# A hybrid decoder block: order of the up projection's first products, slots for value weights, three stages for down's weight sums, and down's first operands during up

## The chip, the cores and the metric

The kernel runs on one core of one Trainium2 chip. The metric is device time in microseconds, the median of several executions. Five engines work beside each other: TensorE (PE) multiplies and transposes, ScalarE (ACT) and VectorE (DVE) work elementwise, GpSimd (POOL) takes a few subtractions, and SyncE (SP) issues all transfers in its own order. Each engine takes its instructions in program order.

## What is computed

One decoder block on 1024 rows of width 1024, in float32:

```python
h = rms_norm(x, norm_mix_w)
q_nsa, kv_nsa, g_nsa, q_ret, k_ret, v_ret, g_ret, g_merge = jnp.split(h @ w_in, split_at, axis=-1)
y_a = nsa_attention(...) @ w_nsa_branch                  # 512 -> 1024
y_b = gated_norm(retention(...)) @ w_ret_branch          # 1024 -> 1024
gate_a, gate_b = jnp.split(jax.nn.sigmoid(g_merge), 2, axis=-1)
x = x + (gate_a * y_a + gate_b * y_b) @ w_mix_out        # 1024 -> 1024
h = rms_norm(x, norm_ffn_w)
u = causal_dwconv(h @ w_ffn_up)                          # 1024 -> 2 x 2816, width 3
u_gate, u_val = jnp.split(u, 2, axis=-1)
x = x + (jax.nn.silu(u_gate) * u_val) @ w_ffn_down       # 2816 -> 1024
return rms_norm(x, norm_final_w)
```

## The kernel before, in words

**Splits.** Every matrix product is made of three products of two parts: `split` (L175, L176) makes a high part on ScalarE (a copy into the product's type) and a low part on VectorE or GpSimd (source minus high part). High by high, high by low and low by high are added up in PSUM (`mm3`, L283 in the profile). A weight block is 128 x 1024 floats, 512 KB; it is loaded into `wr`, a buffer with two slots (`wraw`), and split into `wh` and `wl` (`wpool`, five slots of each).

**Order.** A scheduler sets the order of each engine from the program, as far as data and buffer slots allow; only TensorE's order from the second half of mix to the first products of up is the order of the code (`pe_order`).

**Branch stage.** The loop over `ch` and `i` (L1000 to L1018) makes eight attention rows: the gate row `gated(j)` (L978, a load; L979, a sigmoid) is multiplied on VectorE with the row's product (L1012), and the retention output is transposed and split into `orT`. A second loop does the same for eight retention rows with `w_b`, adds the attention rows `ma` and splits the sum into `mh`, `ml`.

**Sums of down's weights.** Up and down are each done with seven products of halves instead of eight (a Winograd form), which needs sums of operands. `t_sums(j, x, y)` makes those of down's weights for step j of 11: four loads of 256 KB (L989, L990) into `tq`, four subtractions on VectorE (L992 to L995), four stores (L997) to `t0` to `t3` in device memory. Before, six of the 11 stand in the attention rows, five in the first half of mix.

**Mix.** Two halves of `w_mix` in four weight blocks each (`Weights`: L202 load, L209 high part, L215 low part). In the second half each finished row is normalised (`end_row`), and `piece` transposes it and copies it (L1087, L1090), makes its low part (L1091) and, for rows 4 to 7, the sums of halves (L1098 to L1101, two of the four on GpSimd but in the last row).

**Up.** 22 filters f, each with seven products of 512 columns in a row of banks. `sums` splits the row sums into `bht`, `blt` (L175, L176). The first five filters (`LEAD`) begin early: `first_weights` loads and splits the gate half of a filter's weights, `start_up` multiplies it and copies the product (L1186, `c` from `f`), and only then the next product may be added to that bank. `other_weights` loads the value half and makes sums of both halves on VectorE (L1214 to L1220). `up` does the other products; `conv` (L1230 on ScalarE, L1231 and L1232 on VectorE) convolves the two results, and their product (L1259) is stored (L1261) as `act`.

**Down.** Units (product i, step j) take activations `a` (two loads L1290, split `sh`, `sl`) and weights. `prepared` fetches both, two units ahead. The tail is not touched by the change, but that `a11` is loaded once more.

Of the kernel before, what the change touches and what calls it, by code (L numbers as in the profile page):

```python
# [18 lines left out]
P = 128  # L19
D = 1024  # L20
S = 1024
# [142 lines left out]
def hybrid_block(ctx: ExitStack, tc: tile.TileContext, a, c, out):  # L164
# [839 lines left out]
    for ch in range(2):  # L1004
        nx = Weights(w_a, 0, 4, [(512, 512)]) if ch == 0 else Weights(w_b, 0, KT, [(0, 512)])
        for i in range(4):
# [7 lines left out]
            if len(t_left) > 5:  # L1014
                x, y = ([q[:, 0:512], q[:, 512:S]] for q in
                        (mp.tile([P, S], F32, name="tq", tag="gb", bufs=3) for _ in range(2)))
                t_sums(t_left.pop(0), x, y)
            transposed_split(ps1, o_r[ch * 4 + i], *orT, ch * 4 + i)  # L1018
        gw = nx
    with ort:  # L1020
# [8 lines left out]
        for ch in range(2):  # L1029
            nx = Weights(w_b, 0, KT, [(512, 512)]) if ch == 0 else Weights(w_mix, 0, KT, [(0, 512)])  # L1030
            for i in range(4):
# [10 lines left out]
                ml.append(mlj)  # L1042
            gw = nx
# [34 lines left out]
    def piece(t, h):  # L1078
# [43 lines left out]
    for t in range(NT):  # L1122
        residual(t, 0)
        if t in (1, 3, 5, 6, 7) and len(t_left):
# [42 lines left out]
    def raw_up(f, i):  # L1167
        r = wraw.tile([P, 2, 512], F32, name="wr")
        nc.sync.dma_start(r.rearrange("p a b -> p (a b)"), a["w_ffn_up"][f][:, i * 1024:(i + 1) * 1024])
        return r  # L1170

    def first_weights(f):

        g = raw_up(f, 0)
        p = parts2(g, nc.gpsimd)
        return {k: [x[:, i] for x in p] for i, k in enumerate(("a11", "a12"))}, g
# [26 lines left out]
    cpool = ups.enter_context(tc.tile_pool(name="cp", bufs=8, reuse_waits="tile"))  # L1203
# [6 lines left out]
    def other_weights(f, w, g=None):  # L1210
        v = raw_up(f, 1)
        g = g or raw_up(f, 0)
# [22 lines left out]
    def up(f, w, begun=None):  # L1235
        x, p1 = begun or start_up(w)
# [12 lines left out]
        if not begun:  # L1249
            prod(x, w["a12"], "21", False, True)  # L1250
# [12 lines left out]
    def weights(f):  # L1263
        if f in uw:
            return other_weights(f, uw.pop(f))
        return other_weights(f, *first_weights(f))

    nx = weights(0)
# [7 lines left out]
    STEPS = [(j, min(2, HT - j)) for j in range(0, HT, 2)]  # L1276
    NS = len(STEPS)
# [5 lines left out]
    W = {"b11": (0, 0), "b21": (1, 0), "b22": (1, 1)}  # L1283
    A = {"a11": (0, 0), "a12": (1, 0), "a21": (0, 1), "a22": (1, 1)}
    kept = {}

    def fetch_a(k, i, dst):
# [3 lines left out]
        return dst  # L1291

# [33 lines left out]
    def prepared(sk, tk, i):  # L1326
        j, n = STEPS[i]
        t = wraw.tile([P, 2, 512], F32, name="wr")
        if tk in W:
            kh, nh = W[tk]  # L1330
            r0 = (kh * HT + j) * P
            src = w_dn[r0:r0 + n * P, nh * 512:nh * 512 + 512].rearrange("(k p) n -> p k n", p=P)
        else:
            src = t_d[int(tk[1]) - 1][j:j + n].rearrange("k p n -> p k n")
# [153 lines left out]
```

## Time and profile before

| | us |
|---|---|
| median of 3 executions | 1814.02 (1811.32 to 1814.24) |
| profiled execution | 1812.5 |
| its span in the trace | 1810.7 |
| TensorE busy | 1750.6 |
| VectorE busy | 1186.5 |
| ScalarE busy | 804.2 |
| GpSimd busy | 126.6 |

The span is what the trace covers of the profiled execution. TensorE has work in nearly all of it, so the views to read are those that tell where it has none: its instructions with the idle time ahead of each and the instruction that ended it. All times below are microseconds from the span's start.

### The profile page before, as it was taken

The numbers are of one execution on the slowest core, as the hardware profiler recorded it, in microseconds if no ns is written. First come the engines' busy times: TensorE is split into PE (matmuls) and PEld (weight loads), VectorE is DVE, ScalarE is ACT, GpSimd is POOL, SyncE is SP. The second block draws the span as 40 slices with busy tenths as digits, with TensorE's granted clock in tenths as the row PEclk, the third lists the DMA queues.
The fourth block names the chain that finished last, engine by engine and source line by source line (L and its number), as shares of the span: only waits on it lengthen the run. The fifth ranks groups of instructions, "written<-read, shape, count | busy, mean of one in ns | idle before, by whom it ended". The sixth has DMA issues, their size and how long they took to land.

```text
span 1810.7 us, 22500 instructions
## 1 busy us (share of the span) xinstructions
PE 1750.6 (97%) x8331; PEld 1434.6 (79%) x8331; DVE 1186.5 (66%) x2337; ACT 804.2 (44%) x1464; POOL 126.6 (7%) x78
## 2 busy tenths in 40 slices
PE   7999999999999999999989999789999999999998
PEld 6987888888788888888868877667888888878886
DVE  7445877777875554455644446767767777678666
ACT  6334666666662344136332215434444444343344
POOL 0000020110100000000000002301121211000000
PEclk9999999999999999999989999899999999999999
DMA  6121010110202111101682383322322322395353
GB/s 227 55 82 53 19 56 32 36 59 18 71 24 94 47 37 57 47 1 47 231 270 93 93 300 137 99 70 70 104 71 82 93 70 87 108 354 189 94 163 111
DMA packets 87418, 178.88 MB, mean 99 GB/s; under 512 B 8508, under 2 KB 18316, under 8 KB 87308
## 3 DMA queue, kind: packets, MB, share of 16 engines
q1 hardware_dynamic: 87308, 177.44, 30.2%
q8 instruction: 65, 1.06, 0.2%
q14 instruction: 45, 0.37, 0.1%
HBM read 137.57 MB, written 39.85 MB: 98 GB/s over the span
## 4 chain that ended last, share of the span: by engine, by line
PE 60%; DVE 5%; DMA 4%; ACT 2%; issue 2%; SPq 1%; POOL 1%; DVEq 0%; POOLq 0%; ACTq 0%
PE f L283 33%; PE mm L283 19%; PE fill L772 2%; DMA tq<-in_w_ffn_down 2%; PE po L826 1%; PE pv L718 1%; PE pt L706 1%; PE sc L610 1%; DMA wr<-in_w_ffn_up 1%; PE pst L826 1%; DMA wr<-in_w_mix_out 0%; ACT wh L209 0%; PE pss L871 0%; DVE c L1231 0%; DVE c L1232 0%
## 5 line engine op out<-in xcount | busy, mean ns | idle before, releaser
L283 PE MATMUL mm<-wh,hh 128*128 128x512 f32 (+1 forms) x576 | 224.0, 389 | 0.5 <-ACT hh L175 0.5
L283 PE MATMUL mm<-wh,hl 128*128 128x512 f32 (+1 forms) x576 | 219.8, 382 | 0.0
L283 PE MATMUL mm<-wl,hh 128*128 128x512 f32 (+1 forms) x576 | 219.8, 382 | 0.0
L209 ACT ACTIVATE wh<-wr 128x1024 fp32r<-128x1024 f32 (+1 forms) x72 | 74.6, 1037 | 167.0 <-PE mm L283 83.2
L713 DVE TENSOR_TENSOR pl<-pt,ph 128x512 fp32r<-128x512 f32 (+1 forms) x148 | 100.6, 686 | 41.8 <-ACT ph L710 41.2
L283 PEld LDWEIGHTS mm<-wh,hl 128*128 128x128 f32 x576 | 108.8, 189 | 20.6 <-DVE hl L176 0.3
L283 PEld LDWEIGHTS mm<-wh,hh 128*128 128x128 f32 x576 | 108.8, 189 | 20.2 <-ACT hh L175 0.9
L283 PE MATMUL f<-wh,sh 128*128 128x512 f32 x308 | 121.6, 395 | 3.3 <-ACT sh L175 3.3
L710 ACT ACTIVATE ph<-pt 128x512 fp32r<-128x512 f32 (+1 forms) x148 | 87.7, 594 | 82.8 <-PE pt L706 74.5
L283 PEld LDWEIGHTS mm<-wl,hh 128*128 128x128 f32 x576 | 108.9, 189 | 19.5 <-DVE wl L215 0.5
L283 PE MATMUL f<-wl,sh 128*128 128x512 f32 x308 | 121.5, 395 | 0.0
L283 PE MATMUL f<-wh,sl 128*128 128x512 f32 x308 | 120.7, 395 | 0.0
L283 PE MATMUL f<-bh,wh 128*128 128x512 f32 x264 | 105.0, 398 | 11.9 <-ACT c L1186 11.9
L176 POOL TENSOR_TENSOR wl<-wr,wh 128x1024 fp32r<-128x1024 f32 x22 | 53.6, 2438 | 898.3 <-ACT wh L175 883.4
L283 PE MATMUL f<-bht,wh 128*128 128x512 f32 x264 | 104.8, 397 | 8.3 <-ACT wh L175 8.3
L772 PE MATMUL fill<-hh,wh 128*128 128x512 f32 x256 | 104.5, 408 | 3.0 <-ACT sg L784 2.0
L283 PE MATMUL f<-bht,wl 128*128 128x512 f32 x264 | 105.0, 398 | 2.2 <-DVE wl L176 2.2
L628 ACT ACTIVATE big<-big,st 128x640 f32<-128x640 f32 (+7 forms) x128 | 93.4, 730 | 28.1 <-DVE st L624 27.3
L215 DVE TENSOR_TENSOR wl<-wr,wh 128x1024 fp32r<-128x1024 f32 (+1 forms) x60 | 71.5, 1193 | 51.2 <-ACT wh L209 50.2
L283 PE MATMUL f<-blt,wh 128*128 128x512 f32 x264 | 104.4, 395 | 0.0
L283 PE MATMUL f<-bl,wh 128*128 128x512 f32 x264 | 104.1, 394 | 0.0
L283 PE MATMUL f<-bh,wl 128*128 128x512 f32 x264 | 103.4, 393 | 0.0
(282 smaller groups left out, 4127.6 us busy)
## 6 DMA issues: line engine op xcount, KB each, us to landing
wr<-in_w_ffn_up SPq DMA_DIRECT2D x49, 512.0 KB, 4.7
wr<-in_w_in SPq DMA_DIRECT2D x40, 512.0 KB, 3.7
tq<-in_w_ffn_down SPq DMA_DIRECT2D x44, 256.0 KB, 4.7
t<-tq SPq DMA_DIRECT2D x44, 256.0 KB, 3.0
act<-c SPq DMA_DIRECT2D x22, 512.0 KB, 2.8
wr<-t SPq DMA_DIRECT2D x20, 512.0 KB, 3.5
a<-act SPq DMA_DIRECT2D x33, 256.0 KB, 6.0
gate<-sg SPq DMA_DIRECT2D x32, 256.0 KB, 2.0
```

The lines of the kernel that those rows point to most:

```text
L176: (engine or nc.vector).tensor_tensor(lo, src, f32(hi), OP.subtract)
L209: nc.scalar.activation(hi[:, :, :self.n], self.raw[len(self.hi)], AF.Copy)
L215: self.engine.tensor_tensor(lo[:, :, :self.n], self.raw[j], f32(self.hi[j][:, :, :self.n]), OP.subtract)
L283: nc.tensor.matmul(ps, stat(sp, kt), mov(mp, kt), start=(first and n == 0), stop=(last and n == 3 * nk - 1), skip_group_check=more)
L610: nc.tensor.matmul(out[:, c0:c0 + n], q[:, h, :], mov, start=(q is box["h"]), stop=(q is box["l"]))
L628: nc.scalar.activation(probs[b][h], probs[b][h], AF.Exp, scale=-1.0, bias=stat["nm", b][:, h:h + 1], accum_out=stat["w", b][:, h:h + 1])
L706: nc.tensor.transpose(bx["pt"][:rows, h, :], probs[h][:, k * P:k * P + rows], ident)
L710: nc.scalar.activation(bx["h"][:rows], bx["pt"][:rows], AF.Copy)
L713: nc.vector.tensor_tensor(bx["l"][:rows], bx["pt"][:rows], f32(bx["h"][:rows]), OP.subtract)
L718: nc.tensor.matmul(acc["pv"], v, bx[part][:rows].rearrange("p h q -> p (h q)"), start=start, stop=stop)
L772: nc.tensor.matmul(fx["ps"], w.at(sp, kt, i * P, P), hT[mp][:, kt, half * 512:half * 512 + 512], start=(n == 0), stop=(n == 3 * KT - 1))
L826: nc.tensor.matmul(ps[:, h, :], stat[sp][:, h, :], mov[mp][:, h, :], start=(first and n == 0), stop=(last and n == 2))
```

## The change

It has four parts. The sums of down's weights are made in three stages: four in the attention rows (even rows), three in the retention rows (j = 2, 4, 6, in buffers of attention rows already added), four in the first half of mix. The splits of the row sums of up stand behind the loop of the first five filters in the program, and `piece` makes all four subtractions on VectorE. The value half of up's weights gets a buffer of its own (`v`, two slots), the general buffer `c4` has 6 slots for 8; the second sum is made in place in `wr`, and filters 5 to 21 load their gate half a second time for it. The operands of down's unit (0, 0) are loaded and split before the last filter of up, through `wr` and `wh`, `wl`; the first step of `a11` is loaded again for the third product.

```diff
-            if len(t_left) > 5:
+            if (ch * 4 + i) % 2 == 0:
...
+                if j in (2, 4, 6):
+                    x, y = ([q[:, 0:512], q[:, 512:S]] for q in
+                            (mp.tile([P, S], F32, name="tq", tag=f"ma{j - k}") for k in (2, 1)))
+                    t_sums(t_left.pop(0), x, y)
...
-        side = nc.vector if t == NT - 1 else nc.gpsimd
         nc.vector.tensor_tensor(b11, b12, b11, OP.subtract)
-        side.tensor_tensor(b12, b22, b12, OP.subtract)
+        nc.vector.tensor_tensor(b12, b22, b12, OP.subtract)
         nc.vector.tensor_tensor(b22, b22, b11, OP.subtract)
-        side.tensor_tensor(b21, b21, b22, OP.subtract)
+        nc.vector.tensor_tensor(b21, b21, b22, OP.subtract)
...
-        if t in (1, 3, 5, 6, 7) and len(t_left):
+        if t in (0, 1, 2, 4):
...
-    sums([4, 5])
-    uw, begun = {}, {}
+    fw, begun = {}, {}
     for f in range(LEAD):
-        uw[f], _ = first_weights(f)
-        begun[f] = start_up(uw[f])
+        fw[f] = first_weights(f)
+        begun[f] = start_up(fw[f])
         if f in (0, 2):
-            t = waiting[0][0]
             piece(*waiting.pop(0))
-            sums([t])
-        prod(begun[f][0], uw[f]["a12"], "21", False, True)
+        prod(begun[f][0], fw[f]["a12"], "21", False, True)
+    sums([4, 5, 6])
+    sums([7])
...
-    cpool = ups.enter_context(tc.tile_pool(name="cp", bufs=8, reuse_waits="tile"))
+    cpool = ups.enter_context(tc.tile_pool(name="cp", bufs=6, reuse_waits="tile"))
...
-        v = raw_up(f, 1)
-        g = g or raw_up(f, 0)
+        v = cpool.tile([P, 2, 512], F32, name="v", bufs=2)
+        nc.sync.dma_start(v.rearrange("p a b -> p (a b)"), a["w_ffn_up"][f][:, 1024:])
+        g = raw_up(f)
...
-        s2 = c4()
-        nc.vector.tensor_sub(s2[:, 0], g[:, 0], v[:, 0])
-        nc.vector.tensor_sub(s2[:, 1], g[:, 1], s[:, 1])
-        p = parts2(s2, nc.vector)
+        nc.vector.tensor_sub(g[:, 0], g[:, 0], v[:, 0])
+        nc.vector.tensor_sub(g[:, 1], g[:, 1], s[:, 1])
+        p = parts2(g, nc.vector)
...
+    ready = {}
+    nx = other_weights(0)
     for f in range(FT):
-        w, nx = nx, weights(f + 1) if f + 1 < FT else None
-        up(f, w, begun.pop(f, None))
+        w, nx = nx, None
+        if f + 1 < FT:
+            if f + 1 >= LEAD:
+                fw[f + 1] = first_weights(f + 1)
+            nx = other_weights(f + 1)
+        if f == FT - 1:
+            s = fetch_a("a11", 0, wraw.tile([P, 2, 512], F32, name="wr"))
+            ready[0, 0] = [parts2(s, nc.vector), parts2(fetch_t("b11", 0), nc.vector)]
+        up(f, w)
...
-    ready = {}
...
         if i == 1:
+            held("a11", j)
             held("a21", j)
             held("a22", j)
```

`fetch_t` holds the weight load that stood in `prepared`; `STEPS`, `W`, `A` and `fetch_a` stand earlier in the program and are otherwise the same.

**What moves in the order, 1.** SyncE's queue in the attention rows. `ma4`, `ma5` and `ma6` are the gate loads of the fifth, sixth and seventh row (from `gate4` to `gate6`), `tq` the loads of sums, `t0` to `t3` their stores, `wr` weight blocks of the retention rows. Before:

```order
L202 DMA wr_8790<-in_w_ret_branch 128x2x512
L978 DMA ma4_8796<-gate4_1647 128x1024
L997 DMA t2_8525<-tq_8744 128x512
L989 DMA tq_8825<-in_w_ffn_down 128x512
L997 DMA t1_8524<-tq_8745 128x512
L997 DMA t3_8526<-tq_8745 128x512
L990 DMA tq_8825<-in_w_ffn_down 128x512
L989 DMA tq_8826<-in_w_ffn_down 128x512
L990 DMA tq_8826<-in_w_ffn_down 128x512
L978 DMA ma5_8853<-gate5_1648 128x1024
```

With the change:

```order
L202 DMA wr_8756<-in_w_ret_branch 128x2x512
L978 DMA ma4_8768<-gate4_1647 128x1024
L202 DMA wr_8762<-in_w_ret_branch 128x2x512
L989 DMA tq_8797<-in_w_ffn_down 128x512
L990 DMA tq_8797<-in_w_ffn_down 128x512
L989 DMA tq_8798<-in_w_ffn_down 128x512
L990 DMA tq_8798<-in_w_ffn_down 128x512
L978 DMA ma5_8825<-gate5_1648 128x1024
L997 DMA t0_8523<-tq_8797 128x512
L978 DMA ma6_8868<-gate6_1649 128x1024
```

Between the fifth and the sixth row's gate stood three stores and four loads of two different sums; now there are four loads of one, and the seventh gate follows behind one store.

**What moves in the order, 2.** ScalarE at the start of up. `c2` from `f` is the copy of the first product (L1186 before, L1188 now), `bht` from `pc` are the splits of sums, `wh` from `wr` that of a weight block, `rs_s` and `h` belong to the last row's norm. Before:

```order
L175 ACTIVATE bht2_10398<-pc_10282 128x4x128
L175 ACTIVATE bht2_10398<-pc_10351 128x4x128
L256 ACTIVATE h_10373,ss_10374<-c2_10324 128x512
L175 ACTIVATE bht3_10400<-pc_10275 128x4x128
L233 ACTIVATE rs_s_10379<-rs_v_10377 128x1
L175 ACTIVATE bht3_10400<-pc_10344 128x4x128
L175 ACTIVATE bht1_10402<-pc_10007 128x4x128
L175 ACTIVATE bht1_10402<-pc_10074 128x4x128
L175 ACTIVATE bht4_10404<-pc_10016 128x4x128
L175 ACTIVATE bht4_10404<-pc_10083 128x4x128
L1186 ACTIVATE c2_10441<-f_10428 128x512
```

With the change:

```order
L175 ACTIVATE bht2_10396<-pc_10280 128x4x128
L175 ACTIVATE wh_10492<-wr_10490 128x1024
L256 ACTIVATE h_10371,ss_10372<-c2_10322 128x512
L175 ACTIVATE bht2_10396<-pc_10349 128x4x128
L175 ACTIVATE bht3_10398<-pc_10273 128x4x128
L233 ACTIVATE rs_s_10377<-rs_v_10375 128x1
L1188 ACTIVATE c2_10423<-f_10410 128x512
```

The copy stands ahead of five splits that it followed, and behind one split of weights (`wh_10492`) that was not there.

**What moves in the order, 3.** VectorE at the step from up to down. L1255 (now L1257) ends the last filter's last product, L1231 and L1232 (now L1233 and L1234) are its convolutions, L1259 (now L1261) their product; `sl` are low parts of down's activations, `wl` of its weights. Before:

```order
L1255 TENSOR_TENSOR c4_13476<-f_13463,c2_13446 128x512
L176 TENSOR_TENSOR wl_13671<-wr_13661,wh_13670 128x1024
L176 TENSOR_TENSOR sl_13563<-a11_0_13559,sh_13562 128x1024
L1231 SCALAR_TENSOR_TENSOR c4_13518<-c4_13476,cw_65,c4_13518 128x1023
L1231 SCALAR_TENSOR_TENSOR c4_13523<-c4_13477,cw_65,c4_13523 128x1023
L1232 SCALAR_TENSOR_TENSOR c4_13518<-c4_13476,cw_65,c4_13518 128x1022
L1232 SCALAR_TENSOR_TENSOR c4_13523<-c4_13477,cw_65,c4_13523 128x1022
L176 TENSOR_TENSOR sl_13576<-a11_1_13572,sh_13575 128x1024
L1259 TENSOR_TENSOR c4_13518<-c4_13518,c4_13523 128x1024
```

With the change:

```order
L1257 TENSOR_TENSOR c4_13499<-f_13486,c2_13469 128x512
L176 TENSOR_TENSOR wl_13644<-wr_13634,wh_13643 128x1024
L1233 SCALAR_TENSOR_TENSOR c4_13541<-c4_13499,cw_65,c4_13541 128x1023
L1233 SCALAR_TENSOR_TENSOR c4_13546<-c4_13500,cw_65,c4_13546 128x1023
L1234 SCALAR_TENSOR_TENSOR c4_13541<-c4_13499,cw_65,c4_13541 128x1022
L1234 SCALAR_TENSOR_TENSOR c4_13546<-c4_13500,cw_65,c4_13546 128x1022
L176 TENSOR_TENSOR sl_13586<-a11_1_13582,sh_13585 128x1024
L1261 TENSOR_TENSOR c4_13541<-c4_13541,c4_13546 128x1024
```

The low part of step 0 is gone from this place; that of step 1 stands behind the convolutions, as before.

## Rows read from the trace of the kernel before

**Rows 1.** The page, part 1: engine, busy us, share of the span, instructions.

```profile
PE 1750.6 (97%) x8331; PEld 1434.6 (79%) x8331; DVE 1186.5 (66%) x2337; ACT 804.2 (44%) x1464; POOL 126.6 (7%) x78
```

**Rows 2.** TensorE by line, 880 to 960: count | busy, mean | idle before, releaser.

```profile
L283 PE MATMUL mm<-oaT,wh 128*128 128x512 f32 x107 | 35.5, 413 | 2.2 <-DVE ma L1012 2.2
...
L283 PE MATMUL mm<-orT,wh 128*128 128x512 f32 x58 | 21.6, 451 | 2.6 <-DVE ma L1012 2.6
...
L275 PE MATMUL tp<-ident,big 128*128 128x128 f32 x56 | 7.9, 286 | 3.0 <-DVE orT L176 3.0
```

**Rows 3.** Table by stretches: length, busy time (instructions) by engine, PEclk, DMA share, GB/s.

```profile
880.00:920.00 40.00, 35.70 (x175) 29.08 (x174) 27.22 (x37) 14.74 (x22) 0.00 (x0) 0.93 0.91 307
920.00:960.00 40.00, 36.47 (x134) 27.23 (x133) 15.31 (x17) 9.37 (x10) 0.00 (x0) 0.86 0.64 219
960.00:1030.00 70.00, 70.00 (x310) 57.91 (x309) 31.98 (x27) 19.89 (x19) 0.00 (x0) 1.00 0.24 78
1060.00:1090.00 30.00, 27.08 (x118) 21.46 (x117) 16.61 (x29) 6.93 (x12) 0.00 (x0) 1.00 0.90 304
1125.00:1150.00 25.00, 14.89 (x55) 11.60 (x54) 22.56 (x31) 13.40 (x25) 13.22 (x8) 0.80 0.25 81
1185.00:1240.00 55.00, 44.51 (x173) 33.73 (x172) 41.05 (x48) 21.71 (x23) 4.12 (x3) 0.94 0.26 87
1240.00:1585.00 345.00, 345.00 (x1496) 280.35 (x1494) 252.33 (x287) 147.50 (x160) 60.53 (x34) 1.00 0.27 86
```

**Rows 4.** Timeline of SyncE's queue, branch stage: start, us of issuing.

```profile
917.53 0.45 SPq L978 DMA_DIRECT2D ma<-gate  x1
```

**Rows 5.** Timeline of TensorE, mix stage: start, us, [idle before, releaser].

```profile
1078.68 0.49 PE L283 MATMUL f<-wh,mh 128*128 128x512 f32 x1 [2.15 <-ACT wh L209]
```

**Rows 6.** Timeline of VectorE, mix stage.

```profile
1069.30 0.69 DVE L993 TENSOR_TENSOR tq<-tq 128x512 f32<-128x512 f32 x1 [4.67 <-DMA tq<-in_w_ffn_down]
```

**Rows 7.** TensorE, start of up: by line from 1125 to 1185, then timeline.

```profile
L283 PE MATMUL f<-bh,wh 128*128 128x512 f32 x44 | 19.3, 438 | 11.9 <-ACT c L1186 11.9
...
1136.29 0.80 PE L283 MATMUL f<-bh,wh 128*128 128x512 f32 x1 [7.04 <-ACT c L1186]
...
1146.69 0.80 PE L283 MATMUL f<-bh,wh 128*128 128x512 f32 x1 [3.07 <-ACT c L1186]
```

**Rows 8.** Timeline of ScalarE, start of up.

```profile
1130.34 0.63 ACT L175 ACTIVATE bht<-pc 128x512 fp32r<-128x512 f32 x1 [4.25 <-DVE pc L1100]
...
1133.07 2.69 ACT L175 ACTIVATE bht<-pc 128x512 fp32r<-128x512 f32 x5
1135.67 0.57 ACT L1186 ACTIVATE c<-f 128x512 f32<-128x512 f32 x1
```

**Rows 9.** Timeline of GpSimd and of VectorE, start of up.

```profile
1123.42 2.42 POOL L176 TENSOR_TENSOR wl<-wr,wh 128x1024 fp32r<-128x1024 f32 x1 [1.02 <-ACT wh L175]
...
1129.61 0.69 DVE L1100 TENSOR_TENSOR pc<-pc 128x512 f32<-128x512 f32 x1 [0.85 <-POOL pc L1099]
```

**Rows 10.** TensorE by line, first filters of up, 1185 to 1240.

```profile
L283 PE MATMUL f<-bht,wh 128*128 128x512 f32 x38 | 15.6, 411 | 8.3 <-ACT wh L175 8.3
L283 PE MATMUL f<-bht,wl 128*128 128x512 f32 x37 | 15.2, 412 | 2.2 <-DVE wl L176 2.2
```

**Rows 11.** Timeline of VectorE, one filter of up.

```profile
1418.82 1.22 DVE L1259 TENSOR_TENSOR c<-c,c 128x1024 f32<-128x1024 f32 x1
...
1437.74 1.22 DVE L1259 TENSOR_TENSOR c<-c,c 128x1024 f32<-128x1024 f32 x1
...
1442.61 1.22 DVE L176 TENSOR_TENSOR wl<-c,wh 128x1024 fp32r<-128x1024 f32 x1
```

**Rows 12.** Timeline of TensorE and of VectorE, first unit of down.

```profile
1588.50 0.50 PE L283 MATMUL f<-wh,sh 128*128 128x512 f32 x1 [3.26 <-ACT sh L175]
...
1589.62 2.48 DVE L1231 SCALAR_TENSOR_TENSOR c<-c,cw,c 128x1023 f32<-128x1023 f32 x2
```

**Rows 13.** The page, part 6: loads of up's weights, count, KB, median us to landing.

```profile
wr<-in_w_ffn_up SPq DMA_DIRECT2D x49, 512.0 KB, 4.7
```

More of the change, by code (lines that the diff above doesn't have):

```diff
@@ L1165, in parts2, with raw_up @@
         return hi, lo
-    def raw_up(f, i):
+    def raw_up(f):
         r = wraw.tile([P, 2, 512], F32, name="wr")
-        nc.sync.dma_start(r.rearrange("p a b -> p (a b)"), a["w_ffn_up"][f][:, i * 1024:(i + 1) * 1024])
+        nc.sync.dma_start(r.rearrange("p a b -> p (a b)"), a["w_ffn_up"][f][:, 0:1024])
         return r
     def first_weights(f):
-        g = raw_up(f, 0)
-        p = parts2(g, nc.gpsimd)
-        return {k: [x[:, i] for x in p] for i, k in enumerate(("a11", "a12"))}, g
+        p = parts2(raw_up(f), nc.gpsimd)
+        return {k: [x[:, i] for x in p] for i, k in enumerate(("a11", "a12"))}
     def prod(ps, w, k, first=True, last=True):
@@ L1208, in hybrid_block, with other_weights @@
     act_d = [dram.tile([P, 2, 512], F32, name=f"act{f}") for f in range(FT)]
-    def other_weights(f, w, g=None):
-        v = raw_up(f, 1)
-        g = g or raw_up(f, 0)
+    def other_weights(f):
+        w = {}
+        v = cpool.tile([P, 2, 512], F32, name="v", bufs=2)
+        nc.sync.dma_start(v.rearrange("p a b -> p (a b)"), a["w_ffn_up"][f][:, 1024:])
+        g = raw_up(f)
         s = c4()
@@ L1233, in conv, with up @@
         return y
-    def up(f, w, begun=None):
-        x, p1 = begun or start_up(w)
+    def up(f, w):
+        x, p1 = begun.pop(f, None) or start_up(fw[f])
         y = bank()
@@ L1248, in up @@
         nc.vector.tensor_add(cv[:, 1], z, u3)
-        if not begun:
-            prod(x, w["a12"], "21", False, True)
+        if f >= LEAD:
+            prod(x, fw[f]["a12"], "21", False, True)
         nc.scalar.activation(cg[:, 0], x, AF.Copy)
@@ L1261, in up, with fetch_a, fetch_t @@
         nc.sync.dma_start(act_d[f], yg)
[L1263 to L1268, printed above, removed]
-    for f in range(FT):
-        w, nx = nx, weights(f + 1) if f + 1 < FT else None
-        up(f, w, begun.pop(f, None))
+    STEPS = [(j, min(2, HT - j)) for j in range(0, HT, 2)]
+    NS = len(STEPS)
+    A = {"a11": (0, 0), "a12": (1, 0), "a21": (0, 1), "a22": (1, 1)}
+    W = {"b11": (0, 0), "b21": (1, 0), "b22": (1, 1)}
+    def fetch_a(k, i, dst):
+        (kh, sh), (j, n) = A[k], STEPS[i]
+        for x in range(n):
+            nc.sync.dma_start(dst[:, x], act_d[kh * HT + j + x][:, sh])
+        return dst
+    def fetch_t(k, i):
+        j, n = STEPS[i]
+        t = wraw.tile([P, 2, 512], F32, name="wr")
+        if k in W:
+            kh, nh = W[k]
+            r0 = (kh * HT + j) * P
+            src = w_dn[r0:r0 + n * P, nh * 512:nh * 512 + 512].rearrange("(k p) n -> p k n", p=P)
+        else:
+            src = t_d[int(k[1]) - 1][j:j + n].rearrange("k p n -> p k n")
+        nc.sync.dma_start(t[:, :n], src)
+        return t
+    ready = {}
+    nx = other_weights(0)
+    for f in range(FT):
+        w, nx = nx, None
[7 more added lines that the diff above has]
+        up(f, w)
     tp.close()
     ups.close()
-    STEPS = [(j, min(2, HT - j)) for j in range(0, HT, 2)]
-    NS = len(STEPS)
     keep = ctx.enter_context(tc.tile_pool(name="keep", bufs=1, side="right", reuse_waits="tile"))
@@ L1282, in hybrid_block @@
     kp2 = ctx.enter_context(tc.tile_pool(name="keep2", bufs=1, reuse_waits="tile"))
-    W = {"b11": (0, 0), "b21": (1, 0), "b22": (1, 1)}
-    A = {"a11": (0, 0), "a12": (1, 0), "a21": (0, 1), "a22": (1, 1)}
     kept = {}
-    def fetch_a(k, i, dst):
-        (kh, sh), (j, n) = A[k], STEPS[i]
-        for x in range(n):
-            nc.sync.dma_start(dst[:, x], act_d[kh * HT + j + x][:, sh])
-        return dst
     def held(k, i):
@@ L1326, in prepared @@
     def prepared(sk, tk, i):
[L1327 to L1334, printed above, removed]
-        nc.sync.dma_start(t[:, :n], src)
+        n = STEPS[i][1]
+        t = fetch_t(tk, i)
         s = S_OF[sk](i)
```

## The prediction, before any run of the change

> **What bounds the kernel now.** Read the page first, for the engine that has no room: TensorE is busy 97% of the span [rows 1]. A shorter time can therefore come only from TensorE's idle time and from stretches in which its clock is low; the change leaves its 8331 products and transposes alone. The second view is TensorE's instructions grouped by line, stretch by stretch, with the idle time ahead of them and who ended it; the third is the table by stretches, with granted clock and DMA share. The diff touches nothing before about 880 us, and five places after it have idle time.
>
> The branch stage, where attention rows become merged rows, idles 2.2 + 2.6 + 3.0 = 7.8 us, all of it waiting for VectorE [rows 2]. Its clock is also down: a mean of 0.93 over one 40-us stretch and 0.86 over the next, so between its two levels of 2.4 and 1.2 GHz, and 1.00 in the 70 us behind, where TensorE has no idle time [rows 3]. The mix stage idles 2.2 us for a weight split [rows 5]. The start of the up projection idles 11.9 us for ScalarE's copy of a first product: 7.0, 3.1, and 1.8 in two more waits [rows 7]. Its first filters idle 8.3 + 2.2 us for ScalarE's and VectorE's weight splits [rows 10]. From 1240 to 1585 TensorE never idles [rows 3]. The step into down idles 3.3 us [rows 12]. To judge one edit, ask whether it moves the instruction that ends such a wait.
>
> **Sums of down's weights, fewer in the branch stage.** A sum is four loads, four 0.69-us subtractions [rows 6] and four stores of 256 KB: 2.1 MB. Six stood in the eight attention rows, now four; three go into the retention rows, four instead of five stay in mix. The stores stand on SyncE's queue, each waiting for its subtraction, and the gate loads stand behind them: the sixth row's gate was issued only at 917.53 [rows 4], near the middle of the two stretches that idle. VectorE's product with the gate, and its splits, came late by that; TensorE waited. With a sum in every second row a gate has at most one sum's stores ahead of it, and the stage moves 4.2 MB less of 21 (307 GB/s for 40 us and 219 for 40 [rows 3]). I follow the eight gates down the new queue, with the old durations of issue and landing, and find each issued a row before its use: all 7.8 us go. The bounds are 4 (two waits stay, as the stage's first 40 us have a DMA share of 0.91 [rows 3]) and 7.8. The clock lost (1 - 0.93) x 40 + (1 - 0.86) x 40 = 8.4 us of work; some of that low clock lay in idle time, counted already, so I take 6.0, between 0 (it stays low for another reason) and 8.4. Together 13.8.
>
> The three sums moved into the retention rows cost 3 x 4 x 0.69 = 8.3 us of VectorE. They lie in a stretch of 70 us in which VectorE works 32 and the DMA share is 0.24, while TensorE works all 70 [rows 3]: cost 0. If a load were late in front of a row's product, each could cost up to one landing, 4.7 us [rows 13], so 14 at the most.
>
> **Mix.** TensorE's 2.2 us come from the last weight block of the second half: VectorE stood 4.67 us for a sum's load and kept the weight's split behind it [rows 5, 6]. The fourth sum still stands ahead of that block in both queues; only the fifth is gone. I take half, 1.1, between 0 and 2.2. The row of this stretch is a DMA share of 0.90 at 304 GB/s [rows 3], so a sum less does little more than move the same bytes. The Trainium skill (DMA: Bandwidth & Descriptors, "Where 436 GB/s comes from") puts the ceiling of the fabric at 435 GB/s; by it 304 leaves room, the wait would be one of order alone, all 2.2 would go and the sum below would be 1.1 larger. The rows of the stretch neither reach that rate nor show that it can't be reached; I keep the value from the row.
>
> **Start of up.** ScalarE works in order. The first copy (0.57 us, 1135.67) stands behind eight splits of sums; one waited 4.25 us for a VectorE subtraction [rows 8], which itself waited for one of GpSimd [rows 9], and five more took 2.69 [rows 8]. Now the copy has three split rows ahead, but also one new wait: the next filter's weight split, whose load waits for GpSimd's previous split, over at 1123.42 + 2.42 = 1125.8 [rows 9]. Plus a landing of 4.7 [rows 13] gives 1130.5; a double-width split (1.1, twice the 2.69/5 = 0.54 of a single one), a square of single width and two splits (three times 0.54) bring the copy to 1133.3 and TensorE back at 1133.9 instead of 1136.29: 2.4. The second copy again has a weight split ahead of it: GpSimd works from 1131.6 to 1134.0, the load behind it lands at 1138.7, the split ends at 1139.8, five sum splits (2.7) and the copy (0.6) at 1143.1. TensorE wants it 1146.69 - 3.07 - 1136.29 = 7.3 us after the restart, at 1141.2. A wait of 1.9 replaces 3.1: 1.2. Of the last two waits (1.8) I take 0.8; what remains is the copy itself. The six GpSimd subtractions become six of 0.69 on VectorE, 4.1 us; each takes the place of a wait, such as the 0.85 us ahead of a 0.69-us step [rows 9], so they count as 0. Idle gain 4.4. The clock of 0.80 over 25 us [rows 3] covers mostly idle; I add 0.6. Together 5.0, between 2 (landings of 7) and 8.
>
> **Own slots for the value weights.** They free the two-slot raw buffer, which starts loads earlier, and 17 filters load their gate half a second time: 512 KB beside the 18.9 us of a filter [rows 11], at a DMA share of 0.27 [rows 3]. That is hidden. What ends the first filters' waits is a split, and the split waits for sums on VectorE that still stand behind the convolution of the filter before (two 2.48-us pairs, as [rows 12] has them); the order of VectorE is the same here. So I expect 0.5 of 10.5; bounds -2 (a smaller general pool, 6 slots for 8) and 10.5 plus the clock's 3.3 (0.94 over 55 us [rows 3]).
>
> **First operands of down made during up.** The wait of 3.3 us [rows 12] was for the split of the first activations. Now their unit, 24 products of 345 / 1496 = 0.23 us [rows 3], or 5.5 us, can follow up at once, from 1588.50 - 3.26 = 1585.2 until 1590.7. The next unit's eight first products last 1.8 us more, until 1592.5, and then want a low part that VectorE makes only after the last convolution: its two 2.48-us pairs formerly came after that split, from 1589.62 [rows 12], and now come before it. Without a double-width split on ScalarE and one on VectorE ahead of them (1.1 + 1.2) they run from 1587.3 to 1592.3, and the low part ends near 1593.5. A new wait of 1.0 is late next: 2.3 gained, between 0 and 3.3. The operand is loaded a second time, 512 KB, during the second product of down; it is wanted only in the third, so that costs nothing.
>
> **Sum.** 13.8 + 0 + 1.1 + 5.0 + 0.5 + 2.3 = 22.7 us. The profiled execution took 1812.5 (span 1810.7): 1789.8. The median of the three runs is 1.5 above that execution: 1791.3, rounded 1791. About 0.2%, 3.6 us, is what a measurement of this kernel can tell from no change.
>
> **Rivals.**
> (a) The branch stage stays bound by its loads. For it: a DMA share of 0.91 where the first wait is. Against it: the next 40 us have 0.64 and idle 3.5 us against 4.3, behind gates that were issued late [rows 2 to 4]. Gain there 4 and no clock instead of 13.8: 12.9 in all, 1801.
> (b) The buffer slots, not the convolutions, hold the first filters' splits. For it: raw loads wait for a slot there. Against it: VectorE is 41 of 55 us busy [rows 3] and has the same order. Then 10.5 + 3.3 come on top: about 36 in all, 1778.
> (c) The change does not do what it says: the copy stands ahead of splits in the list, but the weight split in front waits for its load (landing of 7 instead of 4.7), and TensorE starts at 1136 again. Gain 22.7 - 5.0 = 17.7: 1796.
> (d) Slower. The second gate load of every filter takes one of the two raw slots, and its slot comes free only with VectorE's split at 1442.61 + 1.22 = 1443.8; VectorE wants the data shortly before its product of two convolutions, one filter (1437.74 - 1418.82 = 18.9) after 1437.74, so at about 1456 [rows 11]. That is 12.2 us for a landing of 4.7 [rows 13]. If it took longer, every one of 17 filters would stall by the excess; from 22.7 / 17 = 1.3 us, that is a landing of 13.5, the gain is gone, and at 15 the time is 1791 + 17 x 2.8 = 1839. For it: only that these loads queue behind an activation store. Against it: a DMA share of 0.27.
>
> **How the numbers follow.** Forecast 0.63, (a) 0.13, (b) 0.11, (c) 0.07, (d) 0.04, a loss spread over the retention rows that eats the rest 0.02. The range runs from rival (b), 1778, to beyond (a) with the start of up as in (c), 1806; it leaves out (d) and little else. Faster by over 0.2%: all but (d) and the spread loss, and a little of (a) with every other bound low: 0.92; within 0.2%: 0.03; slower: 0.05.
>
> **What would show it.** Right: no idle time of TensorE over 0.5 us between 880 and 960, with a granted clock of 0.98 or more there; the sixth gate issued before 905, where 917.53 stood; still none between 960 and 1030; the first copy at 1133 counted on the old clock, with a wait near 4.6; waits of some 10 us in the first filters; no wait at the start of down but one of about 1 us in its second unit. Wrong: a clock under 0.95 in the branch stage without waits; waits for a sum's load in the retention rows; any idle time of TensorE in the filters past the fifth.

## The result, and the profile after

The changed kernel takes 1786.87 us (1785.60 to 1788.55, 4 runs), the kernel before 1814.13 (4 runs): a ratio of 0.9854, interval 0.9837 to 0.9871. The forecast was 1791, range 1778 to 1806. The profiled execution took 1786.91, its span is 1785.1: 25.6 us less than before.

The page of the changed kernel, part 1, answers to [rows 1]: as many instructions on TensorE, 8 us less of busy time, the rest of the gain from its idle time.

```profile
PE 1742.7 (98%) x8331; PEld 1430.9 (80%) x8331; DVE 1189.1 (67%) x2343; ACT 803.9 (45%) x1464; POOL 120.6 (7%) x72
```

The table by stretches answers to [rows 3]. The stretches are as long as those, and moved 10 to 15 us forward so that each holds the same stage. A row gives the stretch, its length, the busy time and instructions of TensorE, its weight loads, VectorE, ScalarE and GpSimd, then the granted clock, the DMA share and GB/s.

```profile
870.00:910.00 40.00, 39.97 (x195) 32.67 (x194) 27.39 (x35) 17.00 (x23) 0.00 (x0) 1.00 0.84 285
910.00:950.00 40.00, 39.74 (x188) 32.71 (x186) 20.30 (x24) 13.98 (x17) 0.00 (x0) 1.00 0.63 210
950.00:1020.00 70.00, 70.00 (x310) 57.82 (x309) 40.08 (x38) 19.23 (x19) 0.00 (x0) 1.00 0.51 171
1050.00:1080.00 30.00, 27.80 (x117) 21.99 (x116) 15.21 (x28) 10.19 (x20) 2.41 (x1) 0.94 0.81 268
1110.00:1135.00 25.00, 19.67 (x86) 15.69 (x86) 24.23 (x34) 14.58 (x28) 8.88 (x3) 0.93 0.36 119
1170.00:1225.00 55.00, 46.44 (x181) 35.68 (x180) 40.50 (x48) 20.93 (x23) 6.27 (x4) 0.94 0.29 96
```

The two branch stretches have no idle time worth naming (0.03 and 0.26 us) and a clock of 1.00, where they had 0.93 and 0.86. The sums moved into the retention rows raise VectorE there from 32 to 40 us and the DMA share from 0.24 to 0.51; TensorE works all 70 us. New is the low clock behind mix (0.94). The gate of the sixth row, at 917.53 in [rows 4], stands on SyncE's queue at:

```profile
902.11 0.45 SPq L978 DMA_DIRECT2D ma<-gate  x1
```

TensorE grouped by line, at the start of up and in the first filters: count | busy, mean | idle before and who ended it ([rows 7] and [rows 10] before):

```profile
L283 PE MATMUL f<-bh,wh 128*128 128x512 f32 x40 | 16.9, 422 | 6.2 <-ACT c L1188 6.2
...
L283 PE MATMUL f<-bht,wl 128*128 128x512 f32 x52 | 21.7, 417 | 4.1 <-DVE wl L176 4.1
L283 PE MATMUL f<-bht,wh 128*128 128x512 f32 x52 | 21.6, 415 | 5.3 <-ACT wh L175 5.3
```

and its timeline where waits are left, [idle before, releaser]: in mix (two), at the first and second copy, and in down's second unit.

```profile
1062.36 0.49 PE L283 MATMUL f<-wh,mh 128*128 128x512 f32 x1 [1.44 <-ACT wh L209]
1063.61 0.51 PE L283 MATMUL f<-wl,mh 128*128 128x512 f32 x1 [0.76 <-DVE wl L215]
...
1116.65 0.50 PE L283 MATMUL f<-bh,wh 128*128 128x512 f32 x1 [2.14 <-ACT c L1188]
...
1125.57 0.50 PE L283 MATMUL f<-bh,wh 128*128 128x512 f32 x1 [3.19 <-ACT c L1188]
...
1570.53 0.50 PE L283 MATMUL f<-wh,sl 128*128 128x512 f32 x1 [0.85 <-DVE sl L176]
```

VectorE's timeline in the first filter, in a late one (the product of convolutions that [rows 11] has at 1437.74), and at the step to down:

```profile
1165.03 2.48 DVE L1233 SCALAR_TENSOR_TENSOR c<-c,cw,c 128x1023 f32<-128x1023 f32 x2 [0.78 <-ACT c L1232]
1167.43 2.47 DVE L1234 SCALAR_TENSOR_TENSOR c<-c,cw,c 128x1022 f32<-128x1022 f32 x2
1169.82 0.69 DVE L1218 TENSOR_TENSOR c<-c,wr 128x512 f32<-128x512 f32 x1
...
1171.62 1.22 DVE L1261 TENSOR_TENSOR c<-c,c 128x1024 f32<-128x1024 f32 x1
...
1414.86 1.22 DVE L1261 TENSOR_TENSOR c<-c,c 128x1024 f32<-128x1024 f32 x1
...
1564.48 2.48 DVE L1233 SCALAR_TENSOR_TENSOR c<-c,cw,c 128x1023 f32<-128x1023 f32 x2
1566.88 2.47 DVE L1234 SCALAR_TENSOR_TENSOR c<-c,cw,c 128x1022 f32<-128x1022 f32 x2
1569.26 1.22 DVE L176 TENSOR_TENSOR sl<-a,sh 128x1024 fp32r<-128x1024 f32 x1
```

Time marks carry the account by stages: when TensorE begins the same product in both traces. One ahead of the branch waits begins at 906.93 before and at 907.29 now, 0.4 us later. One of the retention rows begins at 948.01 and 932.39, 15.6 us earlier. TensorE stops for the first copy at 1136.29 - 7.04 = 1129.25 before [rows 7] and at 1116.65 - 2.14 = 1114.51 now: 14.7 us are gained by then. A product behind the start of up begins at 1180.30 and 1158.40: 21.9. The late filter's mark shows 1437.74 - 1414.86 = 22.9 us, the span 25.6.

| stage | forecast | measured |
|---|---|---|
| ahead of the branch stage | 0 | -0.4 |
| branch and retention rows | 13.8 | 16.0: from -0.4 to 15.6; idle 7.8 to 0.3, clock 8.4 to 0 |
| mix | 1.1 | -0.9: from 15.6 to 14.7 |
| start of up | 5.0 | 7.2: from 14.7 to 21.9 |
| first filters | 0.5 | 1.0: from 21.9 to 22.9 |
| step to down and the end | 2.3 | 2.7: from 22.9 to 25.6 |
| sum | 22.7 | 25.6 |

### The profile page after: what moved, and what is told of

It reads as the page before. It is cut to its first block, busy times and chain, and to the rows that moved or that the text cites. A ratio compares the mean times of both kernels' runs of the same rounds, so it can differ in the third digit from the quotient of the medians.

```text
span 1785.1 us, 22560 instructions
## 1 busy us (share of the span) xinstructions
PE 1742.7 (98%) x8331; PEld 1430.9 (80%) x8331; DVE 1189.1 (67%) x2343; ACT 803.9 (45%) x1464; POOL 120.6 (7%) x72
## 5 line engine op out<-in xcount | busy, mean ns | idle before, releaser
L209 ACT ACTIVATE wh<-wr 128x1024 fp32r<-128x1024 f32 (+1 forms) x72 | 74.6, 1037 | 154.9 <-PE mm L283 76.8
L175 ACT ACTIVATE wh<-wr 128x1024 fp32r<-128x1024 f32 (+1 forms) x87 | 88.3, 1020 | 102.5 <-PE f L283 49.7
```

The source lines that it names most:

```text
L175: nc.scalar.activation(hi, src, AF.Copy)
L209: nc.scalar.activation(hi[:, :, :self.n], self.raw[len(self.hi)], AF.Copy)
```

## The experiments

All are timed against the kernel before on their chip; its median was 1811.5 in the first job, 1813.3 in the second and 1813.2 in the third. Executions of one kernel spread by up to 9 us, so single waits are read from the traces and only large steps from the times. A time set beside the changed kernel's 1786.9 comes from another job than that one, and each trace is one execution.

**The sums put back.** Edit on the changed kernel:

```diff
-            if (ch * 4 + i) % 2 == 0:
+            if len(t_left) > 5:
...
-                if j in (2, 4, 6):
...
-        if t in (0, 1, 2, 4):
+        if t in (1, 3, 5, 6, 7) and len(t_left):
```

> The changed kernel (1786.9) with the sums of down's weights put back where they were: six in the attention rows, none in the retention rows, five in mix. Theory: the sums' place is what took the 7.6 us of idle time and the low clock out of the branch stage. Both return: idle near 7.8 us there, clock about 0.93 and 0.86, and the time is 14 to 17 us above the changed kernel, 1801 to 1804. Rival: the clock of the branch stage is low for a reason of its own, so only the idle time returns: 7 to 8 us, 1794 to 1795.

Measured: 1801.1 us. TensorE by line in the branch stage, and its second stretch:

```profile
L283 PE MATMUL mm<-oaT,wh 128*128 128x512 f32 x114 | 37.9, 415 | 1.5 <-DVE ma L1012 1.5
L283 PE MATMUL mm<-orT,wh 128*128 128x512 f32 x60 | 20.2, 413 | 2.6 <-DVE ma L1012 2.6
L275 PE MATMUL tp<-ident,big 128*128 128x128 f32 x58 | 8.1, 282 | 3.5 <-DVE orT L176 3.5
...
920.00:960.00 40.00, 36.92 (x142) 28.36 (x143) 17.61 (x21) 10.29 (x10) 0.00 (x0) 0.90 0.70 234
```

The waits are back, at the lines and sizes of [rows 2] (7.6 us here, 7.8 there), and the clock falls with them, but less: 0.98 and 0.90 in the two stretches, 4.8 us of work, where the kernel before lost 8.4. The theory holds in kind, at the low end of its times; all four runs, from 1797.5 up, lie above the rival's 1794 to 1795.

**Gates ahead of the sums, in the kernel before.** The same six sums, the same bytes, another place on SyncE's queue:

```diff
+    gates = [gated(j) for j in range(KT)]
     for ch in range(2):
...
-            m = gated(ch * 4 + i)
+            m = gates[ch * 4 + i]
```

> The kernel BEFORE (1814.1) with one thing changed: all eight gate loads of the attention rows are issued before the first row; its six sums stay in the attention rows, so the stage moves the same bytes. Theory: the gates were late because they stood behind the sums' stores on SyncE's queue. Then 10 to 16 us go, 1798 to 1804, and the clock of the stage is 0.97 or more. Rival: the bytes of the stage bind; then the sums' loads and the splits behind them on VectorE are late as before, the idle time stays at 5 us or more and the time at 1808 or above.

Measured: 1800.6 us, ratio to the kernel before 0.9929 (0.9909 to 0.9950). TensorE by line, the two stretches, and SyncE's queue:

```profile
L283 PE MATMUL mm<-orT,wh 128*128 128x512 f32 x100 | 31.2, 392 | 2.0 <-DVE ma L1013 2.0
L275 PE MATMUL tp<-ident,big 128*128 128x128 f32 x64 | 8.4, 272 | 0.0
...
870.00:910.00 40.00, 39.97 (x196) 32.76 (x196) 25.71 (x32) 19.13 (x24) 0.00 (x0) 1.00 0.81 287
910.00:950.00 40.00, 38.04 (x178) 31.05 (x177) 25.37 (x33) 9.47 (x12) 0.00 (x0) 1.00 0.84 284
...
874.66 3.72 SPq L978 DMA_DIRECT2D ma<-gate  x8
```

Both stretches move 284 to 287 GB/s, the stage more in its second half than before (219 [rows 3]), and still 5.8 of 7.8 us of waits and all of the low clock are gone. The bytes didn't bind. What made the branch stage slow was, for all but the 2.0 us that are left, the order of one queue: gate loads behind stores that wait for VectorE. SyncE's own waits in the kernel before, 870 to 950 (us in total, times, longest), show the largest of these:

```profile
SPq L997 <- DVE tq L992: 10.0, 4, 3.8
```

With the other three subtractions the stores stood there 28 us. Moving sums away helped mainly by that, not by the 4.2 MB.

**Four, four and three.** Edit on the changed kernel:

```diff
-                if j in (2, 4, 6):
+                if j in (2, 4, 5, 6):
...
-                            (mp.tile([P, S], F32, name="tq", tag=f"ma{j - k}") for k in (2, 1)))
+                            (mp.tile([P, S], F32, name="tq", tag=f"ma{k}") for k in
+                             {2: (0, 1), 4: (2, 3), 5: (0, 1), 6: (4, 5)}[j]))
...
-        if t in (0, 1, 2, 4):
+        if t in (0, 1, 2):
```

> The changed kernel with the sums at four, four and three: the fourth sum of mix goes into the retention rows (j = 5, in the buffers of the sum of j = 2). Theory: the last weight block of mix waits because this sum stands ahead of it on SyncE's queue and on VectorE; the 2.2 us of idle time in mix and the low clock behind it (0.94 over 30 us) go: 2 to 4 us faster, 1783 to 1785, and the retention rows still never idle. Rival: the bytes bind; the block comes as late as before and the time stays within 1 us of 1786.9.

Measured: 1784.2 us. The table by stretches:

```profile
950.00:1020.00 70.00, 70.00 (x309) 57.81 (x308) 42.42 (x42) 18.91 (x19) 0.00 (x0) 1.00 0.61 202
1020.00:1050.00 30.00, 30.00 (x131) 24.32 (x130) 12.53 (x19) 1.78 (x3) 0.00 (x0) 1.00 0.88 299
1050.00:1080.00 30.00, 30.00 (x139) 24.58 (x138) 14.99 (x33) 12.98 (x27) 2.41 (x1) 1.00 0.59 202
```

Mix has no wait and full clock, the retention rows none either. The stretch ahead of the place still has a DMA share of 0.88 at 299 GB/s (0.88 at 290 in the changed kernel). So here too the wait was one of order: the value taken from the DMA share was the wrong one. The size varies, though. With four sums in mix, seven traces have a first wait of 0 to 1.9 us and always the second of 0.76; with three, three of four traces have neither; and the run with five put back had 0.5 and 0.76. The Trainium skill (DMA: Bandwidth & Descriptors, "Where 436 GB/s comes from") puts the fabric at 435 GB/s, and the limit that binds transfers from device memory at about 358. 304 lies under both, and the trace agrees in that the wait went at 299; it doesn't show either ceiling.

**GpSimd's six subtractions back** (the line with `side` in `piece`, as before).

> The changed kernel with the six subtractions of the row sums on GpSimd again, the order of the splits kept. Theory as predicted: the exchange is worth nothing, since the wait for a weight split's load decides: within 1 us of 1786.9, first waits of up about 2.1 and 3.2 us. Rival: the order alone does little, because the splits that still stand ahead of the copies wait for GpSimd, and GpSimd's weight split waits for them: 3 us or more slower, 1790 and up.

**The order of the splits back** (`sums` called in the loop again, all subtractions on VectorE).

> The changed kernel with the splits of sums called inside the loop of the first five filters again, all subtractions on VectorE. Theory: ScalarE again has eight splits ahead of the first copy, and the start of up waits some 9 to 12 us instead of 6.2: 3 to 6 us slower, 1790 to 1793. Rival: with VectorE making all subtractions the splits no longer wait for them, and the copy stands no later than now: within 1.5 us of 1786.9.

**Both back.**

> The changed kernel with both halves of the second part undone: the splits called in the loop of the first five filters, and six subtractions on GpSimd. Each half undone alone left the waits of the start of up at 6.1 and 6.5 us, against 6.3 with both in place and 11.9 in the kernel before. Theory: either half alone is enough, since what hurt was the chain of both, splits ahead of the copy that wait for GpSimd's steps; with both undone the waits return to 11 to 13 us. Rival: the halves are worth nothing, and the waits fell because the stages ahead changed; then they stay at 6 to 7 us.

Measured: 1791.7, 1792.9 and 1791.7 us. TensorE by line at the start of up, first with GpSimd back (and a table row of its first filters):

```profile
L283 PE MATMUL f<-bh,wh 128*128 128x512 f32 x40 | 17.6, 439 | 6.1 <-ACT c L1189 6.1
...
1172.00:1227.00 55.00, 47.25 (x169) 35.63 (x168) 37.47 (x46) 19.85 (x22) 6.23 (x4) 0.84 0.30 96
```

with the order back:

```profile
L283 PE MATMUL f<-bh,wh 128*128 128x512 f32 x40 | 16.9, 423 | 6.5 <-ACT c L1188 6.5
```

and with both:

```profile
L283 PE MATMUL f<-bh,wh 128*128 128x512 f32 x40 | 17.2, 431 | 8.7 <-ACT c L1189 8.7
```

Each half alone leaves the waits where the whole change has them, 6.1 and 6.5 against 6.3; only both together cost 2.4 us of waiting. The six other traces that have this part as the changed kernel has it wait 4.8 to 6.4 us, so 8.7 stands out, though it is one trace, and by their times the three runs can't be told apart. As far as the waits go, the two halves do the same thing twice. And 8.7 is neither the theory's 11 to 13 nor the rival's 6 to 7, nor the 11.9 of the kernel before: in the run with the gates ahead, which touches nothing behind the branch stage, these waits are already shorter:

```profile
L283 PE MATMUL f<-bh,wh 128*128 128x512 f32 x44 | 19.3, 439 | 9.7 <-ACT c L1187 9.7
```

So about 2 of the 5.6 us that these waits lost may have come from the stage ahead; with a spread of 1.6 us between traces of one program part that isn't shown, nor is the step of the chain. As to time, the run with GpSimd back missed its theory and lies where its rival had it, 4.8 us over the changed kernel, but with the same waits, so it is inconclusive. Its trace has a clock of 0.84 in the first filters where the changed kernel had 0.94, 5.5 us over 55, though its waits there are no longer. The run with the order back missed its 9 to 12 us of waits: by the waits its rival was right, though its time, 1792.9, lies where the theory had it.

**Slots back** (value weights in the raw slots, 8 general slots, one gate load).

```diff
-        v = cpool.tile([P, 2, 512], F32, name="v", bufs=2)
+        v = wraw.tile([P, 2, 512], F32, name="wr")
...
-        g = raw_up(f)
+        g = first_raw.pop(f, None) or raw_up(f)
```

> The changed kernel with the value weights in the two raw slots again, 8 slots in the general buffer, the second sum in a slot of its own and one gate load a filter. Theory: the convolution ahead of the sums on VectorE sets the first filters' waits, so the slots are worth 0 to 1 us: 1786 to 1788, waits of some 10 us in the first filters. Rival: the slots are what shortened these waits and more, by their earlier loads: 4 us or more slower, 1791 and up.

Measured: 1789.5 us (1785.9 to 1790.6). TensorE in the first filters:

```profile
L283 PE MATMUL f<-bht,wh 128*128 128x512 f32 x50 | 21.3, 425 | 7.8 <-ACT wh L175 7.8
L283 PE MATMUL f<-bht,wl 128*128 128x512 f32 x50 | 20.6, 412 | 1.7 <-DVE wl L176 1.7
```

9.5 us of waits, as with the slots (9.4). The executions overlap with those of the changed kernel; a loss of some 3 us without them is left open, and the waits show none.

**Weight sums ahead of convolutions.** Edit on the changed kernel: the value weights of filters 2 to 4 are called two filters ahead, just before the convolution.

```diff
+        then()
         yg = conv(cg.rearrange("p a b -> p (a b)"), f)
...
-        up(f, w)
+        up(f, ow[f], lambda: make(f + 2) if f + 2 <= 4 else None)
```

> The changed kernel with the weight sums of filters 2 to 4 called ahead of the convolution of the filter two before, so that VectorE makes them first. Same loads, same slots. Theory: the first filters' 9.4 us of waits are VectorE's convolutions standing ahead of these sums, not loads or slots: 6 to 12 us faster, 1775 to 1781. Rival: the loads land too late for that; the same waits stay and the time is within 1.5 us of 1786.9. A second rival: the convolutions become late and their slots end the waits later on, then the waits appear in filters 5 to 8.

Measured: 1778.2 us, ratio to the kernel before 0.9805 (0.9775 to 0.9835). TensorE by line, and the stretch of the first filters:

```profile
L283 PE MATMUL f<-bht,wl 128*128 128x512 f32 x52 | 20.6, 397 | 1.0 <-DVE wl L176 1.0
L283 PE MATMUL f<-bht,a22h 128*128 128x512 f32 x16 | 7.2, 453 | 2.3 <-DVE c L1246 2.3
...
1170.00:1225.00 55.00, 51.62 (x213) 40.28 (x212) 48.90 (x53) 23.84 (x26) 6.90 (x4) 0.97 0.26 93
```

The waits fall from 9.4 to 3.3 us with the same loads and slots. The edit also issues these loads earlier, but they weren't late: in the changed kernel the gate load that the step at 1169.82 reads was issued at 1148.63, so by the median landing of 4.7 us [rows 13] it was there at about 1153.3 (an estimate), ahead of the convolutions that begin at 1165.03. VectorE's order set the waits. Of what is left, 2.3 us are new: TensorE waits for a sum of products (L1246) that VectorE now makes late, behind convolutions. No wait is new in the filters where the second rival looked for it.

**Down's operands back** (the block at `f == FT - 1` and `held("a11", j)` left out).

> The changed kernel with down's first operands made where they were, after up. Theory: the wait of about 3.3 us for the first split of activations returns, and the wait of 0.85 us in the second unit goes: 2.4 us slower, 1789.3. Rival: the wait only moved, and the time stays within 1 us of 1786.9.

Measured: 1793.5 us (1790.2 to 1797.9). TensorE at the first unit of down:

```profile
1565.04 0.51 PE L283 MATMUL f<-wh,sh 128*128 128x512 f32 x1 [3.31 <-ACT sh L175]
```

The wait of [rows 12] is back and that of the second unit gone: 2.5 us, as expected. The median is 4.2 us above the 1789.3 expected. The waits elsewhere don't explain that. In the profiled execution (1791.5) the clock was 0.88 over 55 us of the first filters, where the changed kernel had 0.94, which is 3.3 us of work; whether it was so in the others isn't known.

**Both moves that gained, together.**

> The changed kernel with both moves that gained alone: sums at four, four and three, and the weight sums of filters 2 to 4 ahead of convolutions. Theory: they touch different waits and add up: no wait in mix, some 3.5 us in the first filters, 1774 to 1777. Rival: the freed time is lost again at the start of up, which then waits longer than 6.3 us: 1778 or more.

Measured: 1776.3 us (1773.6 to 1778.8), ratio to the kernel before 0.9795 (0.9762 to 0.9827): no wait in mix, 3.4 in the first filters, 6.3 at the start of up. The gains add up by the waits; the span, 1776.9, is only 0.8 us under that of the run with the weight sums ahead. One thing that differs between executions is a wait in the branch stage for the convolution's weights, here 1.22 us with 3.4 us of low clock behind it:

```profile
926.84 0.57 PE L1027 MATMUL tp<-ident,wr 44*128 44x44 f32 x2 [1.22 <-DMA wr<-in_ffn_conv_w]
```

The kernel before has none there; the changed kernel's trace has 0.23 us, and the traces of its variants 0 to 1.5. Why it comes wasn't tested. This is the fastest median of the study, within the spread of two others.

**The copies first.** Two versions of that kernel in which ScalarE's order at the start of up is written out, with one and with two free raw slots:

```diff
+    pe_order.enter_context(tc.manual_schedule(engines={PE, ACT}))
+    fw[0] = first_weights(0)
+    fw[1] = first_weights(1)
...
+        if f + 2 < LEAD:
+            fw[f + 2] = first_weights(f + 2)
+        for t in {0: [4], 1: [5], 2: [6], 4: [7]}.get(f, []):
+            sums([t])
...
-    gain2 = wraw.tile([P, 2, 512], F32, name="wr").rearrange("p a b -> p (a b)")
+    gain2 = [mx.tile([P, 512], F32, name="gain2", tag="pc", bufs=16) for _ in range(2)]
```

The last pair of lines is in the version with two slots alone.

> The same written order of ScalarE, the norm gain still in one of the two raw slots. Theory: one slot serves a weight load, a split on ScalarE and a split on GpSimd in a row (4.7 + 1.1 + 2.4 us or more for each filter, against 5.5 us of products), so waits for the second and third filters' weights take the place of those for the copies: no faster than the run with both moves. Rival: order alone is enough, and the time equals that with two slots within 1.5 us.

> The kernel of the run before with ScalarE's order at the start of up written out (each first product's copy ahead of the next splits of sums) and the norm gain of the mix stage moved out of the two raw slots into two buffers of the mix pool, so that two weight loads are under way. Theory: the copies wait only for what stands ahead of them on ScalarE, a weight split that waits for its load; the waits on copies fall from 6.3 to 3 us or less, 3 to 5 us faster than the run before. Rival: the weight splits on GpSimd (2.4 us and more each) come late instead, or the splits of sums do in front of the first filter; then the idle time is as before and the time within 1.5 us.

Measured: 1777.2 us with one slot, 1782.6 with two. TensorE's timeline with one slot, and what VectorE waited for:

```profile
1148.45 0.79 PE L283 MATMUL f<-bht,wh 128*128 128x512 f32 x1 [3.58 <-ACT wh L175]
...
1142.35 2.50 DVE L176 TENSOR_TENSOR blt<-pc,bht 128x512 fp32r<-128x512 f32 x4 [4.94 <-ACT bht L175]
```

and with two:

```profile
1148.86 0.79 PE L283 MATMUL f<-bht,wh 128*128 128x512 f32 x1 [8.19 <-ACT wh L175]
...
1145.14 0.69 DVE L1224 TENSOR_TENSOR c<-v 128x512 f32<-128x512 f32 x1 [4.48 <-DMA v<-in_w_ffn_up]
```

The waits for copies fall to 3.4 us in both (1.4 or 1.3, and three of 0.69), near the 3 or less of the theory for two slots. But the first filter then waits for its own weights, 3.6 us with one slot and 8.2 with two. In both, the written order puts the last four splits of sums behind the last copy, and VectorE stands 4.9 us for them ahead of the first weight sums. With two slots it then stands 4.48 us more for the value load: by the program that load's buffer lies in the memory of the mix stage, and it was issued at 1140.69, when the last low part of the sums ended (1140.66). That this is the whole cause wasn't tested. The theories didn't name that wait; the rival for two slots came near with late splits of sums, but not with the time, 6.3 us over the run with both moves. The theory for one slot was right as to the time and wrong as to which weights are waited for. A copy that comes earlier here only chose which product waits.

## Why the prediction was right, and where its sizes were off

- **The total.** 25.6 us by the span where 22.7 were forecast is nearer than its terms: branch stage and start of up gave 2.2 us more each, mix 2.0 less, so part of the nearness is luck.
- **What bounds.** Right: all of the gain lies at the five places that were read, and the steady filters gained nothing.
- **Branch stage.** The waits went all but 0.3 us, as taken, and the clock gave back all 8.4 us where 6.0 was taken. The low clock came and went with the waits: 4.8 us of it returned with them in the run with the sums back, and all of it left in the one with the gates ahead, though 2.0 us of waits stayed. What the forecast didn't see is the wait for the convolution's weights, up to 1.5 us in the traces of the variants. The mechanism, gates behind stores, is shown by the latter run; rival (a), the bytes, fell there.
- **Retention rows.** Right: cost 0.
- **Mix.** Wrong in sign in this trace. The step that failed is half of 2.2 for one sum less. That wait fell only from 2.2 to 1.4, a second of 0.76 stayed that the forecast hadn't counted, and a low clock of 0.94 over 30 us took 1.8. The run with four, four and three shows the cause: the fourth sum, which the forecast had named as still standing ahead. But the first wait is 0 to 1.9 us in seven traces with four sums, so half of 2.2 is wrong for this execution more than in general.
- **Start of up.** Right in direction, 7.2 us where 5.0 were forecast, with steps that were off. ScalarE's rows show the weight splits and the copy, GpSimd's the weight splits that the two loads wait for:

```profile
1113.32 1.06 ACT L175 ACTIVATE wh<-wr 128x1024 fp32r<-128x1024 f32 x1 [1.97 <-DMA wr<-in_w_ffn_up]
...
1116.02 0.58 ACT L1188 ACTIVATE c<-f 128x512 f32<-128x512 f32 x1
...
1121.38 1.06 ACT L175 ACTIVATE wh<-wr 128x1024 fp32r<-128x1024 f32 x1 [2.29 <-DMA wr<-in_w_ffn_up]
```

```profile
1107.11 2.40 POOL L176 TENSOR_TENSOR wl<-wr,wh 128x1024 fp32r<-128x1024 f32 x1 [33.62 <-ACT wh L175]
1114.45 3.21 POOL L176 TENSOR_TENSOR wl<-wr,wh 128x1024 fp32r<-128x1024 f32 x1 [4.94 <-ACT wh L175]
```

 The first weight split came at 1113.32 where the working gives 1130.5 - 14.7 = 1115.8: GpSimd's split ended at 1109.5 and not at 1125.8 - 14.7 = 1111.1, and the load landed within 3.8 us of that, not 4.7. So the first wait is 2.1, not 4.6. The second is 3.2, not 1.9, though its copy ends 8.9 us after TensorE's restart where 9.2 were forecast: GpSimd's split took 3.21 us and not 2.40, but the load landed in under 3.8. It is TensorE that came sooner, 1122.38 - 1116.65 = 5.7 us after the restart. The 7.3 taken from the kernel before held some 3.3 us at the lower clock (0.50 granted from 1136.30 to 1139.60). So the clock is the term that was too small here: the idle time fell by 5.7 us, from 11.9 to 6.2, and the other 1.5 of the 7.2 are faster work, where 0.6 was taken. And the term was credited to the order alone, while by the waits each half alone does it and the stage ahead may have given some 2 us.
- **First filters.** Right: waits of 9.4 where 10 were forecast, and the reason, the convolutions' place on VectorE, is shown by the run that moved the sums ahead. Rival (b) fell with the slots put back.
- **Down.** Right by its own steps: the wait of 3.3 went, one of 0.85 came at the ninth product of the second unit (forecast 1.0), behind the convolutions.
- **Rivals (c) and (d).** The first copy came earlier, not at the old time. From 1225 to 1560 TensorE works 334.16 of 335 us, and the 0.84 left is one wait at 1230, in the sixth filter, for a low part on VectorE behind the convolutions. So the forecast's sign of an idle time past the fifth filter came, once and small; the kernel before and the run with the slots back have none there, and what brings it wasn't tested. The later filters wait for nothing, so the second gate load costs at most that.

## What to carry to other kernels

A load that the bound engine needs should not stand on its queue behind a store that waits for a slower engine: the same bytes in another order were worth 13 us here. When one engine's order is the cause, move the work that feeds the next stage ahead of work that nobody waits for yet, such as a convolution whose result is only stored. Undo the halves of a change singly and together: here, by the waits of single traces, two halves did the same thing, and each alone looked worthless.

## What was not expected of the hardware

The clock made up a third of the gain: with the waits of the branch stage, none over 2.6 us, went 17 us at half speed, 8.4 us of work. Nearly the same waits don't cost the same clock in every execution: with waits of 9.4 and 8.6 us in the first filters, the changed kernel and the one with GpSimd back had 0.94 and 0.84 there, so a stage with waits spreads the time of a kernel by several us.

A GpSimd subtraction and VectorE's two-input operations hold each other up, by turns. A 128x512 subtraction on VectorE takes 0.69 us alone; beside a GpSimd split, 1122.52 to 1125.34, one took:

```profile
1123.04 2.85 DVE L176 TENSOR_TENSOR blt<-pc,bht 128x512 fp32r<-128x512 f32 x1
```

It ended at 1125.89, 0.55 us after GpSimd's, so by these figures it did its work when GpSimd was done; a second such pair, from 1115.54 to 1118.21 beside a split that ended at 1117.66, has the same 0.55. The other way round, GpSimd's split from 1114.45 took 3.21 us instead of 2.40, while VectorE went on at 0.69 us an operation until 1115.44.
